# A decoder trunk on one core: up projections of three feed-forwards by seven block products instead of eight

## The chip, the cores and the metric

One core of a Trainium2 chip runs the whole kernel. The metric is the device time of one execution in microseconds. The engines are TensorE (PE in the profile; PEld is its weight load), VectorE (DVE), ScalarE (ACT), GpSimd (POOL) and SyncE (SP), whose queue issues nearly all transfers.

## The reference

256 rows of 1024 numbers go through two layers, all in 32-bit floats:

```
x += 1/2 * SwiGLU_1(RMSNorm(x))          # w_ffn1: up 1024 x 5632, down 2816 x 1024
x += W_o(gated sum of three mixers of RMSNorm(x))
x += 1/2 * SwiGLU_2(RMSNorm(x))          # w_ffn2, the same sizes
x += sigmoid(RMSNorm(x) W_pg) * (p W_pp)
```

and a final RMSNorm. `SwiGLU(h)`: `g, u = split(h @ w_up)`, then `(silu(g) * u) @ w_down`. There are so four feed-forwards: w_ffn1 and w_ffn2 in layers 0 and 1.

## The kernel before

Products are made of three matmuls each (`mm3`): every operand is split into a hi part, rounded to the format fp32r, and a lo part, what the rounding left over; hi x hi, hi x lo and lo x hi are added up in PSUM. A weight unit is a tile of 128 x 1024 numbers, 512 KB: `fetch` brings it into a buffer of the pool wraw (four), `split_unit` makes hi on ScalarE (a copy, L201) and lo on VectorE (a subtraction, L202), in the pools wh and wl, five buffers each. For rows the transposed x is kept in hi and lo (`xth`, `xtl`), one tile for each half of 128 rows (t = 0, 1).

A feed-forward runs over 11 blocks (FB) of 256 gate and 256 value columns. A block has four up units q, each with two slices of 128 of the 1024 inner numbers. For each t it makes 4 x 2 x 3 = 24 up matmuls with 512 columns into one PSUM bank (pool pu, two banks). Then `hid` takes Silu of the gate half on ScalarE (L308) and multiplies it by the value half on VectorE (L309); both apply rstd there, the row factor of the norm, as x itself was transposed without it. The down matmuls of the block before follow (24, into four acc banks that stay for the whole feed-forward), then four transposes of the hidden block and its split into hi and lo (L214, L215; tiles fh and fl). The first and the last block go through t = 0 wholly before t = 1, the others alternate.

`square_linear` is the 1024 x 1024 product behind the mixers (w_out) and the one in the ple step (w_ple_gate); its `consume` adds to x (L954, L415). `norm_after` follows: transposes of raw x (L234), gain with hi and lo (L217, L218), sums of squares (L277), and rstd as a power on GpSimd (L224).

The instructions are written in program order; a scheduler that knows tiles and buffers lays down each engine's final order when the kernel is built, and puts in every wait. Pools of buffers are all opened once, at the start.

Of the kernel before, what the change touches and what calls it, by code (L numbers as in the profile page):

```python
# [8 lines left out]
F32 = mybir.dt.float32  # L9
F32R = mybir.dt.float32r  # L10
# [51 lines left out]

SPLIT_AHEAD = 0
LANES = {'a': 1, 'b': 1, 'c': 2}


class Packed:
# [9 lines left out]
    def array(self):  # L77
        return np.concatenate(self.parts)


# [7 lines left out]
def pack(w):  # L88
    out = []
    for i in range(DEPTH):  # L90
# [10 lines left out]
        def ffn(f):  # L101
            up = w[f + "_up"][i].reshape(4, 2, 128, 2, FB, 256)
            for b in range(FB):
                for q in range(4):
                    p.put((f + "_up", b, q), up[q, :, :, :, b, :].reshape(2, 128, 512))
                for g in range(2):
                    p.put((f + "_down", b, g), rows(f + "_down", b * 256 + g * 128, 1, 0, 1024))
# [22 lines left out]
class Build:  # L130
# [73 lines left out]

    def mm3(self, out, ah, al, bh, bl, start, stop):
        mm = self.nc.tensor.matmul
        mm(out, ah, bh, start=start, stop=False)  # L207
        mm(out, ah, bl, start=False, stop=False)  # L208
        mm(out, al, bh, start=False, stop=stop)  # L209

# [40 lines left out]
    def norm_begin_early(self, gcol):  # L251
        self.next = gcol

    def norm_after(self, t, half):
        if half == 0:
            return
        if t == 0:
            self.norm_begin(self.next)
        for h in range(2):
            self.norm_half(t, h)  # L260
            if self.gcol is None:
                s = slice(h * 512, (h + 1) * 512)
                o = self.tmt("o")
                self.nc.vector.tensor_tensor(o, self.x[:, t, s], self.gf[:, s], op=OP.mult)
                self.og[t].append(o)
        self.norm_finish(t)

    def norm_half(self, t, half):
# [19 lines left out]
    def ffn(self, name, gcol_next, mid=None, hook=None):  # L288
        nc = self.nc
        rstd = self.rstd  # L290
        acc = {}

# [12 lines left out]
        def hid(pu, t):  # L305
            sg = self.tm.tile([128, 256], F32, name="sg", tag="tm")
            hd = self.tm.tile([128, 256], F32, name="hd", tag="tm")
            nc.scalar.activation(sg, pu[t][:, 0, :], AF.Silu, scale=rstd[t])  # L308
            nc.vector.scalar_tensor_tensor(hd, pu[t][:, 1, :], rstd[t], sg, op0=OP.mult, op1=OP.mult)  # L309
            return hd  # L310
# [12 lines left out]
        prev = None  # L323
        for b in range(FB):
            pu = [self.pu.tile([128, 2, 256], F32, name="pu") for t in range(2)]
# [15 lines left out]
            for q, t in order:  # L341
                up(q, t)
            hds = [hid(pu, t) for t in range(2)]
            if b < FB - 1:
                if prev is not None:
                    d = down_units(b - 1)
                    for t in range(2):
                        down(b - 1, d, prev, t, b == 1, False)
                pt = self.pt.tile([128, 2, 256], F32, name="pt")
# [3 lines left out]
            else:  # L353
# [9 lines left out]
                turn(0)  # L363
                down(b - 1, d0, prev, 0, False, False)
# [4 lines left out]
                down(b - 1, d0, prev, 1, False, False)  # L369
# [4 lines left out]
            prev = (hh, ll)  # L374

# [545 lines left out]
    def mixer(self, i, gcol_next):  # L921
# [30 lines left out]
        def consume(t, half, ps):  # L952
            xs = self.x[:, t, half * 512:(half + 1) * 512]
            nc.vector.tensor_tensor(xs, xs, ps, op=OP.add)  # L954
            self.norm_after(t, half)

        self.norm_begin_early(gcol_next)
        self.square_linear("w_out", consume)
# [59 lines left out]
    def program(self, out):  # L1018
# [34 lines left out]
        for i in range(DEPTH):  # L1053
            self.layer = i
            self.ffn("w_ffn1", cols["norm_mix"] + 8 * i, hook=self.late_loads if i == 0 else None)
            self.mixer(i, cols["norm_ffn2"] + 8 * i)
            self.ffn("w_ffn2", cols["norm_ple"] + 8 * i, mid=lambda: self.ple_proj(i))
            if i + 1 == DEPTH:
                self.gf = self.ar1.tile([128, 1024], F32, name="gf", tag="ar1a")
# [3 lines left out]
            self.ple(i, cols["norm_ffn1"] + 8 if i + 1 < DEPTH else None)  # L1063
        for t in range(2):
# [12 lines left out]

def build(nc, aps, out, where):
    from contextlib import ExitStack
    with tile.TileContext(nc) as tc, ExitStack() as es:  # L1080
# [40 lines left out]
```

## Time and profile before

| | us |
|---|---|
| median of three runs | 1531.94 (1531.2 to 1532.58) |
| the profiled execution | 1531.52 |
| its span, first to last instruction | 1529.7 |
| TensorE busy | 1507.0 |
| VectorE busy | 946.2 |
| ScalarE busy | 860.9 |

The page gives busy times by engine, slices of the span, a chain of work that ended last, groups of instructions by source line, and transfers. Matmuls overlap one another, so the duration of one (0.39 us) is longer than the step from one to the next. A line such as L202 can be that of a helper that many stages call. The four feed-forwards lie at about 15 to 200, 560 to 740, 770 to 955 and 1306 to 1490 us of the span.

### The profile page before, as it was taken

What the parts mean: (1) busy time and instruction counts of PE and PEld (TensorE: products, weight loads), DVE (VectorE), ACT (ScalarE), POOL (GpSimd) and SP (SyncE); (2) the same over time, 40 slices, a digit from 0 to 9 for tenths busy, and PEclk for the clock granted to TensorE, in tenths of its full rate; (3) what the DMA queues carried; (4) which work ended last, traced back from release to release, by engine and by line L of the source; (5) the groups of instructions that cost most, each with busy time, mean ns of one, the idle gap of its engine ahead of it and who ended that gap; (6) DMA issues with size and microseconds to landing.
All of it is one profiled execution on the core that took longest, in us unless ns stands there. A gap on an engine that the chain in (4) does not pass through costs nothing.

```text
span 1529.7 us, 21640 instructions
## 1 busy us (share of the span) xinstructions
PE 1507.0 (99%) x8264; PEld 1256.8 (82%) x8264; DVE 946.2 (62%) x1534; ACT 860.9 (56%) x1313; POOL 36.3 (2%) x48
## 2 busy tenths in 40 slices
PE   7999999999999999999999999999999999999997
PEld 6888888888888888888888888888888888888886
DVE  6555577677765665555765456676776566655456
ACT  6444486568655464444764445865775644644455
POOL 0000010000000000000000000100000000000000
PEclk9999999999999999999999999999999999999999
DMA  8565545344535556565565555554353365566652
GB/s 296 187 195 191 185 140 187 123 159 138 172 110 166 192 191 184 180 196 172 184 198 190 191 181 159 183 160 134 126 186 126 127 204 190 174 195 187 190 172 97
DMA packets 76472, 264.54 MB, mean 173 GB/s; under 512 B 8608, under 2 KB 9536, under 8 KB 76368
## 3 DMA queue, kind: packets, MB, share of 16 engines
q1 hardware_dynamic: 76144, 263.00, 53.8%
q8 instruction: 65, 1.06, 0.3%
q0 software_dynamic: 80, 0.11, 0.1%
q14 instruction: 39, 0.32, 0.1%
q10 hardware_dynamic: 144, 0.05, 0.0%
HBM read 262.08 MB, written 1.05 MB: 172 GB/s over the span
## 4 chain that ended last, share of the span: by engine, by line
PE 89%; ACT 5%; DVE 2%; DMA 1%; issue 1%; POOL 0%; SPq 0%; POOLq 0%; ACTq 0%; DVEq 0%
PE pu L207 20%; PE pu L208 20%; PE pu L209 20%; PE acc L209 5%; PE acc L208 5%; PE acc L207 5%; PE sq L207 2%; PE sq L208 2%; PE sq L209 2%; ACT h L201 1%; PE pt L314 1%; DMA raw<-in_weights_dram 1%; PE pt L234 1%; DVE l L202 1%; ACT P L513 1%
## 5 line engine op out<-in xcount | busy, mean ns | idle before, releaser
L202 DVE TENSOR_TENSOR l<-raw,h 128x1024 fp32r<-128x1024 f32 (+3 forms) x512 | 600.0, 1185 | 388.7 <-ACT h L201 382.7
L201 ACT CAST h<-raw 128x1024 fp32r<-128x1024 f32 (+1 forms) x511 | 512.9, 1016 | 375.5 <-PE pu L209 240.0
L207 PE MATMUL pu<-h,xth 128*128 128x512 f32 (+3 forms) x1376 | 534.6, 389 | 8.0 <-DVE h L201 5.9
L208 PE MATMUL pu<-l,xth 128*128 128x512 f32 (+3 forms) x1376 | 526.2, 382 | 2.1 <-DVE l L202 2.1
L209 PE MATMUL pu<-h,xtl 128*128 128x512 f32 (+3 forms) x1376 | 523.5, 381 | 0.0
L207 PEld LDWEIGHTS pu<-h,xth 128*128 128x128 f32 x1376 | 259.4, 189 | 54.6 <-ACT xth L217 5.9
L208 PEld LDWEIGHTS pu<-l,xth 128*128 128x128 f32 x1376 | 259.5, 189 | 46.6 <-DVE l L202 4.8
L209 PEld LDWEIGHTS pu<-h,xtl 128*128 128x128 f32 x1376 | 259.1, 188 | 45.6
L207 PE MATMUL acc<-h,fh 128*128 128x512 f32 x352 | 138.0, 392 | 0.0
L209 PE MATMUL acc<-h,fl 128*128 128x512 f32 x352 | 137.6, 391 | 0.0
L208 PE MATMUL acc<-l,fh 128*128 128x512 f32 x352 | 137.1, 389 | 0.0
L308 ACT ACTIVATE sg<-pu,rstd 128x256 f32<-128x256 f32 x88 | 41.8, 475 | 63.9 <-PE pu L209 63.9
L209 PEld LDWEIGHTS acc<-h,fl 128*128 128x128 f32 x352 | 66.1, 188 | 13.6
L208 PEld LDWEIGHTS acc<-l,fh 128*128 128x128 f32 x352 | 66.1, 188 | 13.4
L207 PEld LDWEIGHTS acc<-h,fh 128*128 128x128 f32 x352 | 66.1, 188 | 13.2
L309 DVE SCALAR_TENSOR_TENSOR hd<-pu,rstd,sg 128x256 f32<-128x256 f32 x88 | 42.3, 481 | 38.7 <-ACT sg L308 38.7
L208 PE MATMUL pu<-l,fh 128*128 128x512 f32 x128 | 50.8, 397 | 0.0
L207 PE MATMUL sq<-h,xth 128*128 128x512 f32 x128 | 50.4, 394 | 0.0
L207 PE MATMUL pu<-h,fh 128*128 128x512 f32 x128 | 50.3, 393 | 0.0
L209 PE MATMUL sq<-h,xtl 128*128 128x512 f32 x128 | 50.0, 391 | 0.0
L208 PE MATMUL sq<-l,xth 128*128 128x512 f32 x128 | 50.0, 391 | 0.0
L217 ACT ACTIVATE xth<-pt,gains 128x128 fp32r<-128x128 f32 x112 | 37.3, 367 | 22.5 <-PE pt L234 11.3
(228 smaller groups left out, 1364.6 us busy)
## 6 DMA issues: line engine op xcount, KB each, us to landing
raw<-in_weights_dram SPq DMA_DIRECT2D x446, 512.0 KB, 4.2
raw<-in_weights_dram SPq DMA_DIRECT2D x48, 384.0 KB, 3.1
raw<-in_weights_dram SPq DMA_DIRECT2D x8, 320.0 KB, 3.0
raw<-in_weights_dram SPq DMA_DIRECT2D x8, 256.0 KB, 2.7
xin<-in_xt_dram SPq DMA_DIRECT2D x4, 256.0 KB, 7.3
x<-in_x_dram SPq DMA_DIRECT2D x2, 512.0 KB, 9.9
out_dram<-o SPq DMA_DIRECT2D x4, 256.0 KB, 2.2
cf<-in_const_f_dram SPq DMA_DIRECT2D x1, 864.0 KB, 8.3
```

The source lines that it names most:

```text
L201: (copy or nc.scalar.copy)(h[:, :m], raw[:, :m])
L202: nc.vector.tensor_tensor(l[:, :m], raw[:, :m], h[:, :m].bitcast(F32), op=OP.subtract)
L207: mm(out, ah, bh, start=start, stop=False)
L208: mm(out, ah, bl, start=False, stop=False)
L209: mm(out, al, bh, start=False, stop=stop)
L217: nc.scalar.activation(h, src, AF.Copy, scale=gain)
L234: nc.tensor.transpose(pt[:, k, :], src[:, half * 512 + k * 128:half * 512 + (k + 1) * 128], self.ident)
L308: nc.scalar.activation(sg, pu[t][:, 0, :], AF.Silu, scale=rstd[t])
L309: nc.vector.scalar_tensor_tensor(hd, pu[t][:, 1, :], rstd[t], sg, op0=OP.mult, op1=OP.mult)
L314: nc.tensor.transpose(pt[:, f, t * 128:(t + 1) * 128], hd[:, f * 128:(f + 1) * 128], self.ident)
L513: nc.scalar.activation(P[n, o], P[n, o], AF.Exp, bias=q[:, 3:4], scale=A_SCALE, accum_out=q[:, 4 + n:5 + n])
```

## The change

In w_ffn2 of both layers and w_ffn1 of layer 1, blocks 1 and 2, 4 and 5, 7 and 8 are joined: a double block is a product of x (two halves of rows, and even and odd slices of 128 of the inner numbers) with weights whose halves are likewise the even and odd slices, and block b and b + 1's 512 + 512 columns as they lie in memory (lo and hi halves of a 1024-wide row). Strassen's method in Winograd's form makes the 2 x 2 product out of seven block products: four sums of x (`sums_x`, once for each feed-forward, behind block 0), four sums of weights (`add`, in place on the raw tiles), and seven `prod`, each of 12 matmuls; three of them gather in the bank pa, whose state in between is copied out (`keep`). Each product makes its own hi and lo parts of its two weight tiles. Weights of a double block come as eight transfers of 512 KB into four tiles of 128 x 2 x 1024 (pools we and wo, two buffers each).

As sums of x mix rows, rstd must be in x before: `scaled_xt` multiplies x by rstd, transposes, multiplies by the gains, and keeps that raw tile for the sums; it stands behind the sum of squares and the power. `hid` then needs no rstd. The pools of the mixers and those of double blocks are opened and closed in turn, on the same memory. w_ffn1 of layer 0 stays as it was, and blocks 0, 3, 6, 9 and 10 of the others are single. The transfer of gf gets a pool of its own. A double block's hidden parts are transposed after the down matmuls of the block before; the next block has down matmuls for two.

```diff
+WIDE = (1, 4, 7)
+def plan(name, i):
+    if (name, i) == ("w_ffn1", 0):
+        return [(False, b) for b in range(FB)]
+    return [(b in WIDE, b) for b in range(FB) if b - 1 not in WIDE]
...
     def norm_after(self, t, half):
+        self.norm_sum(t, half)
+        if self.gcol is None:
+            s = slice(half * 512, (half + 1) * 512)
+            o = self.tmt("o")
+            self.nc.vector.tensor_tensor(o, self.x[:, t, s], self.gf[:, s], op=OP.mult)
+            self.og[t].append(o)
         if half == 0:
             return
-        if t == 0:
-            self.norm_begin(self.next)
-        for h in range(2):
-            self.norm_half(t, h)
...
         self.norm_finish(t)
+        if self.gcol is not None:
+            if t == 0:
+                self.new_xt()
+                self.wide_open()
+            self.scaled_xt(t)
+
+    def scaled_xt(self, t):
+        nc = self.nc
+        raw = self.xr.tile([128, 8, 128], F32, name=f"xr{t}", tag=f"xr{t}")
+        self.rawx[t] = raw
+        xs = [self.tmt("xs") for half in range(2)]
+        nc.scalar.activation(xs[0], self.x[:, t, 0:512], AF.Copy, scale=self.rstd[t])
+        nc.vector.tensor_scalar(xs[1], self.x[:, t, 512:1024], self.rstd[t], None, op0=OP.mult)
+        for half in range(2):
+            pt = self.pt.tile([128, 4, 128], F32, name="pt")
+            for k in range(4):
+                nc.tensor.transpose(pt[:, k, :], xs[half][:, k * 128:(k + 1) * 128], self.ident)
+            c = self.gcol + half * 4
+            g = slice(half * 4, half * 4 + 4)
+            nc.vector.tensor_tensor(raw[:, g, :], pt, self.gains[:, c:c + 4].unsqueeze(2).to_broadcast([128, 4, 128]),
+                                    op=OP.mult)
+            self.hl(self.xth[t][:, g, :], self.xtl[t][:, g, :], raw[:, g, :])
+
+    def wide_open(self):
+        self.scope = ExitStack()
+        for n, bufs in (("we", 2), ("wo", 2), ("xr", 1), ("sx", 1)):
+            setattr(self, n, self.scope.enter_context(self.tc.tile_pool(name=n, bufs=bufs, reuse_waits="tile")))
+        self.rawx = [None, None]
...
+    def sums_x(self):
+        nc = self.nc
+        a = [r.rearrange("p (q k) t -> p q k t", k=2) for r in self.rawx]
+        (a11, a12), (a21, a22) = [(r[:, :, 0, :], r[:, :, 1, :]) for r in a]
+        s1, s2, s3, s4 = [self.tmt("xs").rearrange("p (q t) -> p q t", q=4) for j in range(4)]
+        nc.vector.tensor_tensor(s1, a22, a21, op=OP.subtract)
+        nc.vector.scalar_tensor_tensor(s2, s1, -1.0, a11, op0=OP.mult, op1=OP.subtract)
+        nc.vector.tensor_tensor(s3, a11, a21, op=OP.subtract)
+        nc.vector.scalar_tensor_tensor(s4, a12, -1.0, s2, op0=OP.mult, op1=OP.subtract)
+        self.sx_ = []
+        for j, v in enumerate((s1, s2, s3, s4)):
+            h = self.sx.tile([128, 4, 128], F32R, name=f"sh{j}", tag=f"sh{j}")
+            l = self.sx.tile([128, 4, 128], F32R, name=f"sl{j}", tag=f"sl{j}")
+            self.hl(h, l, v)
+            self.sx_.append((h, l))
...
+    def wide_up(self, name, b):
+        nc = self.nc
+        e, o = self.wide_fetch(name, b)
+        lo, hi = slice(0, 512), slice(512, 1024)
+        pb = self.pu.tile([128, 512], F32, name="pu")
+        pa = self.pu.tile([128, 512], F32, name="pu")
+        pc = self.pt.tile([128, 512], F32, name="pt")
...
+        def prod(ps, st, raws, half, start, stop):
+            for j in range(2):
+                h = self.wh.tile([128, 1024], F32R, name="h").rearrange("p (q n) -> p q n", q=2)
+                l = self.wl.tile([128, 1024], F32R, name="l").rearrange("p (q n) -> p q n", q=2)
+                src = raws[j][:, :, half]
+                nc.scalar.copy(h, src)
+                nc.vector.tensor_tensor(l, src, h.bitcast(F32), op=OP.subtract)
+                for q in range(2):
+                    self.mm3(ps, st[0][:, 2 * j + q, :], st[1][:, 2 * j + q, :], h[:, q, :], l[:, q, :],
+                             start and j == 0 and q == 0, stop and j == 1 and q == 1, True)
+
+        def add(d, dh, r, rh):
+            for j in range(2):
+                nc.vector.tensor_tensor(d[j][:, :, dh], d[j][:, :, dh], r[j][:, :, rh], op=OP.add)
+
+        def keep(ps):
+            c = self.tmt("pc")
+            nc.scalar.copy(c, ps)
+            return c
+
+        mul = nc.vector.scalar_tensor_tensor
+        prod(pa, a11, e, lo, True, False)
+        p1 = keep(pa)
+        add(e, lo, e, hi)
+        prod(pb, s1, e, lo, True, False)
+        p5 = keep(pb)
+        add(e, lo, o, hi)
+        prod(pa, s2, e, lo, False, False)
+        u2 = keep(pa)
+        prod(pb, s4, o, hi, False, True)
+        nc.vector.tensor_tensor(u2, u2, pb, op=OP.add)
+        add(e, hi, o, hi)
+        prod(pa, s3, e, hi, False, False)
+        u3 = keep(pa)
+        prod(pc, a12, o, lo, True, True)
+        nc.vector.tensor_tensor(p1, p1, pc, op=OP.add)
+        nc.scalar.activation(p1, p1, AF.Silu)
+        mul(u2, u2, -1.0, p1, op0=OP.mult, op1=OP.mult)
+        add(e, lo, o, lo)
+        prod(pa, a22, e, lo, False, True)
+        nc.vector.tensor_tensor(p5, p5, u3, op=OP.add)
+        nc.scalar.activation(u3, pa, AF.Silu)
+        mul(p5, p5, -1.0, u3, op0=OP.mult, op1=OP.mult)
+        return [u2, p5]
...
+        for wide, b in plan(name, self.layer):
+            if wide:
+                hds = self.wide_up(name, b)
+                downs()
+                prev = []
+                for j in range(2):
+                    hh = self.fh.tile([128, 2, 256], F32R, name="fh")
+                    ll = self.fl.tile([128, 2, 256], F32R, name="fl")
+                    pt = self.pt.tile([128, 2, 256], F32, name="pt")
+                    for t in range(2):
+                        hid_t(pt, hds[t][:, j * 256:(j + 1) * 256], t)
+                    self.hl(hh, ll, pt)
+                    prev.append((b + j, (hh, ll)))
+                continue
...
             hds = [hid(pu, t) for t in range(2)]
+            if scaled and b == 0:
+                self.sums_x()
...
-POOLS = dict(wraw=4, wh=5, wl=5, act=1, const=1, tm=6, small=4, fh=4, fl=4, ar1=1, ar2=1, pp_=3, gt=6)
+POOLS = dict(wraw=4, wh=5, wl=5, act=1, const=1, tm=6, small=4, fh=4, fl=4)
```

Below, W1 to W14 are the 14 weight tiles that the seven products split, in order.

## Rows read from the trace of the kernel before

**Rows 1.** The page's busy times by engine, and the granted clock in 40 slices of the span (9 is 90% or more).

```profile
PE 1507.0 (99%) x8264; PEld 1256.8 (82%) x8264; DVE 946.2 (62%) x1534; ACT 860.9 (56%) x1313; POOL 36.3 (2%) x48
PEclk9999999999999999999999999999999999999999
```

**Rows 2.** Windows inside three of the four feed-forwards: start and end, length, busy time of each engine with instructions, granted clock, DMA share, GB/s.

```profile
20.00:190.00 170.00, 170.00 (x772) 140.61 (x771) 92.21 (x97) 79.41 (x97) 0.00 (x0) 1.00 0.61 197
560.00:730.00 170.00, 170.00 (x772) 140.56 (x771) 91.16 (x96) 77.52 (x94) 0.00 (x0) 1.00 0.61 190
...
1330.00:1480.00 150.00, 150.00 (x680) 124.15 (x679) 77.22 (x80) 66.87 (x80) 0.00 (x0) 1.00 0.60 183
```

**Rows 3.** The page's groups by line: shapes and count, busy us, mean ns of one, then idle time of the engine before them and what ended it.

```profile
L202 DVE TENSOR_TENSOR l<-raw,h 128x1024 fp32r<-128x1024 f32 (+3 forms) x512 | 600.0, 1185 | 388.7 <-ACT h L201 382.7
L207 PE MATMUL pu<-h,xth 128*128 128x512 f32 (+3 forms) x1376 | 534.6, 389 | 8.0 <-DVE h L201 5.9
```

**Rows 4.** The window of one block of w_ffn2 in layer 1, from its first up matmul to that of the next block; columns as in rows 2.

```profile
1385.32:1402.13 16.81, 16.81 (x80) 13.91 (x78) 8.74 (x9) 7.53 (x10) 0.00 (x0) 1.00 0.61 187
```

**Rows 5.** TensorE's timeline of that block: start, duration, operation; the first and last of 48 up matmuls and of 24 down matmuls (x1 each, a few records missing), the transposes, the next block's first.

```profile
1385.32 0.48 PE L207 MATMUL pu<-h,xth 128*128 128x512 f32 x1
...
1396.11 0.39 PE L209 MATMUL pu<-h,xtl 128*128 128x512 f32 x1
1396.33 0.39 PE L207 MATMUL acc<-h,fh 128*128 128x512 f32 x1
...
1401.55 0.39 PE L209 MATMUL acc<-h,fl 128*128 128x512 f32 x1
1401.78 0.60 PE L314 MATMUL pt<-ident,hd 128*128 128x128 f32 x4
1402.13 0.48 PE L207 MATMUL pu<-h,xth 128*128 128x512 f32 x1
```

**Rows 6.** VectorE's timeline: two lo parts of the next block and fl behind them, one that waits; then two 512-wide operations in a row from a mixer, and three lo parts in a row from the ple step. In brackets the idle time before, and who ended it.

```profile
1385.56 2.36 DVE L202 TENSOR_TENSOR l<-raw,h 128x1024 fp32r<-128x1024 f32 x2 [3.17 <-ACT h L201]
1387.84 0.68 DVE L215 TENSOR_TENSOR fl<-pt,fh 128x512 fp32r<-128x512 f32 x1
1389.46 1.23 DVE L202 TENSOR_TENSOR l<-raw,h 128x1024 fp32r<-128x1024 f32 x1 [0.94 <-ACT h L201]
...
1169.12 0.68 DVE L658 TENSOR_TENSOR e<-e,pt 128x512 f32<-128x512 f32 x1
1169.72 0.68 DVE L659 TENSOR_TENSOR sig<-sig,pt 128x512 f32<-128x512 f32 x1
...
1508.12 3.49 DVE L202 TENSOR_TENSOR l<-raw,h 128x1024 fp32r<-128x1024 f32 x3
```

**Rows 7.** ScalarE's timeline over the same block.

```profile
1384.48 2.00 ACT L201 CAST h<-raw 128x1024 fp32r<-128x1024 f32 x2 [3.35 <-PE acc L209]
1386.38 0.58 ACT L214 CAST fh<-pt 128x512 fp32r<-128x512 f32 x1
1388.37 1.05 ACT L201 CAST h<-raw 128x1024 fp32r<-128x1024 f32 x1 [1.42 <-PE pu L209]
```

**Rows 8.** The timeline of all engines at the end of w_out in layer 1: transposes of raw x, the addition to x of t = 0, its square, sum, mean and power, two of ScalarE's casts, and the last matmul of t = 1.

```profile
1299.45 0.60 PE L234 MATMUL pt<-ident,x 128*128 128x128 f32 x4
1299.65 0.69 DVE L954 TENSOR_TENSOR x<-x,sq 128x512 f32<-128x512 f32 x1 [2.71 <-PE sq L209]
1300.37 0.63 ACT L277 ACTIVATE jk<-x 128x512 f32<-128x512 f32 x1
1301.12 0.16 DVE L282 TENSOR_TENSOR s<-ss 128x1 f32<-128x1 f32 x1 [0.29 <-ACT jk L277]
1301.55 0.56 POOL L224 TENSOR_TENSOR rstd<-ms,mhalf 128x1 f32<-128x1 f32 x1 [118.27 <-DVE ms L223]
1304.06 2.03 ACT L201 CAST h<-raw 128x1024 fp32r<-128x1024 f32 x2
1305.67 0.39 PE L209 MATMUL sq<-h,xtl 128*128 128x512 f32 x1
```

**Rows 9.** The timeline at the end of the ple gate in layer 0, t = 0: sigmoid, product, addition to x, and the power.

```profile
760.32 0.69 ACT L413 ACTIVATE g<-sq,rstd 128x512 f32<-128x512 f32 x1 [3.76 <-PE sq L209]
761.04 0.69 DVE L414 TENSOR_TENSOR g<-g,pp 128x512 f32<-128x512 f32 x1 [2.39 <-ACT g L413]
761.91 0.68 DVE L415 TENSOR_TENSOR x<-x,g 128x512 f32<-128x512 f32 x1
765.53 1.54 POOL L224 TENSOR_TENSOR rstd<-ms,mhalf 128x1 f32<-128x1 f32 x1 [21.00 <-ACT h L201]
```

**Rows 10.** Transfers of weight units (count, KB each, median us from issue to landing), and a window at the start of the kernel (columns as in rows 2).

```profile
raw<-in_weights_dram SPq DMA_DIRECT2D x446, 512.0 KB, 4.2
10.00:15.00 5.00, 3.35 (x7) 2.36 (x8) 3.80 (x9) 4.43 (x8) 0.00 (x0) 1.00 1.04 412
```

**Rows 11.** TensorE's timeline at the start of the kernel.

```profile
11.18 0.79 PE L207 MATMUL pu<-h,xth 128*128 128x512 f32 x1 [1.61 <-ACT h L201]
...
14.32 0.63 PE L209 MATMUL pu<-h,xtl 128*128 128x512 f32 x1
14.74 0.63 PE L207 MATMUL pu<-h,xth 128*128 128x512 f32 x1
...
16.10 0.40 PE L208 MATMUL pu<-l,xth 128*128 128x512 f32 x1
16.34 0.40 PE L209 MATMUL pu<-h,xtl 128*128 128x512 f32 x1
```

More of the change, by code (lines that the diff above doesn't have):

```diff
@@ L1 @@
+from contextlib import ExitStack
 import numpy as np
@@ L102, in ffn @@
             up = w[f + "_up"][i].reshape(4, 2, 128, 2, FB, 256)
+            for wide, b in plan(f, i):
+                if wide:
+                    for k in range(2):
+                        for q in range(4):
+                            p.put((f + "_wide", b, 4 * k + q), up[q, k, :, :, b:b + 2, :].reshape(1, 128, 1024))
+                else:
+                    for q in range(4):
+                        p.put((f + "_up", b, q), up[q, :, :, :, b, :].reshape(2, 128, 512))
             for b in range(FB):
-                for q in range(4):
-                    p.put((f + "_up", b, q), up[q, :, :, :, b, :].reshape(2, 128, 512))
                 for g in range(2):
@@ L252, in norm_begin_early @@
         self.next = gcol
+        self.gcol = gcol
+        self.ss = [self.small.tile([128, 2], F32, name="ss", tag="ss") for t in range(2)]
+        self.rstd = [self.small.tile([128, 1], F32, name="rstd", tag="rstd") for t in range(2)]
     def norm_after(self, t, half):
+        self.norm_sum(t, half)
[4 more added lines that the diff above has]
+            self.og[t].append(o)
@@ new lines, in wide_open, with mixer_open @@
+    def wide_open(self):
[3 more added lines that the diff above has]
+        self.rawx = [None, None]
+    def mixer_open(self):
+        self.scope = ExitStack()
+        for n, bufs in (("ar1", 1), ("ar2", 1), ("pp_", 3), ("gt", 6)):
+            setattr(self, n, self.scope.enter_context(self.tc.tile_pool(name=n, bufs=bufs, reuse_waits="tile")))
@@ new lines, in wide_fetch @@
+    def wide_fetch(self, name, b):
+        out = []
+        for k, pool in enumerate((self.we, self.wo)):
+            for j in range(2):
+                raw = pool.tile([128, 2, 1024], F32, name="wide", tag="wide")
+                for q in range(2):
+                    off, _, m = self.where[self.layer][name + "_wide", b, 4 * k + 2 * j + q]
+                    self.nc.sync.dma_start(raw[:, q, :], self.a[f"weights{self.layer}"][off:off + 128 * m]
+                                           .rearrange("(p m) -> p m", p=128))
+                out.append(raw)
+        return out[:2], out[2:]
@@ L290, in ffn @@
         rstd = self.rstd
+        scaled = (name, self.layer) != ("w_ffn1", 0)
         acc = {}
@@ L323, in ffn, with downs @@
         prev = None
-        for b in range(FB):
+        def downs():
+            for (pb, hT) in prev:
+                d = down_units(pb)
+                for t in range(2):
+                    down(pb, d, hT, t, pb == 0, False)
+        for wide, b in plan(name, self.layer):
+            if wide:
+                hds = self.wide_up(name, b)
+                downs()
+                prev = []
+                for j in range(2):
+                    hh = self.fh.tile([128, 2, 256], F32R, name="fh")
+                    ll = self.fl.tile([128, 2, 256], F32R, name="fl")
+                    pt = self.pt.tile([128, 2, 256], F32, name="pt")
+                    for t in range(2):
+                        hid_t(pt, hds[t][:, j * 256:(j + 1) * 256], t)
+                    self.hl(hh, ll, pt)
+                    prev.append((b + j, (hh, ll)))
+                continue
             pu = [self.pu.tile([128, 2, 256], F32, name="pu") for t in range(2)]
@@ L343, in ffn @@
             hds = [hid(pu, t) for t in range(2)]
+            if scaled and b == 0:
+                self.sums_x()
             if b < FB - 1:
                 if prev is not None:
-                    d = down_units(b - 1)
-                    for t in range(2):
-                        down(b - 1, d, prev, t, b == 1, False)
+                    downs()
                 pt = self.pt.tile([128, 2, 256], F32, name="pt")
@@ L363, in ffn @@
                 turn(0)
-                down(b - 1, d0, prev, 0, False, False)
+                old = prev[0][1]
+                down(b - 1, d0, old, 0, False, False)
                 turn(1)
@@ L368, in ffn @@
                 finish(0)
-                down(b - 1, d0, prev, 1, False, False)
+                down(b - 1, d0, old, 1, False, False)
                 down(b, d1, (hh, ll), 1, False, True)
```

37 lines of the change are left out of this document (23 added, 14 removed).

## The prediction

> **What bounds the kernel now.** I read the page's head first: TensorE is busy for 99% of the span at a granted clock of 0.9 or more in every slice, VectorE 62%, ScalarE 56% [rows 1]. Then the windows of the feed-forward stretches: TensorE is busy 170 of 170 us and 150 of 150 us there, VectorE about half [rows 2]. So inside a feed-forward the stream of matmuls sets the time, and a matmul left out is time gained, as long as its operands are still there in time. The groups by line say who comes next: VectorE's lo parts wait for ScalarE's hi parts, TensorE waits 8 us in all for a hi part, and that over the whole kernel [rows 3]. Next I took one 256-column block apart. It is 16.81 us long, of which VectorE works 8.74 [rows 4]: 48 up matmuls, 24 down matmuls, 4 transposes [rows 5]. From the first down matmul to the last are 23 steps in 5.22 us, 0.227 us each [rows 5]. VectorE and ScalarE sit waiting for TensorE to release a buffer: wh and wl hold five units, and each next hi part starts only when a matmul has ended [rows 6, 7]. These five buffers are the whole lead that the two engines can have.
>
> **What is removed.** A double block is 2 blocks x 48 = 96 up matmuls; seven products of 12 are 84. Nine double blocks (three in each of three feed-forwards) save 9 x 12 x 0.227 = 24.5 us [rows 5]. Down matmuls and transposes keep their number.
>
> [...] The trace shows 227 ns [rows 5], and the sum goes by the trace.
>
> **What is added to VectorE, per double block.** Before, the up part needed 8 lo parts. Now each of the 7 products splits its own two 1024-column tiles: 14 lo parts; and the weight sums take 8 additions of the same shape. A lo part lasts 1.22 us alone, but two in a row take 2.36 and three 3.49, so one more costs 1.14 [rows 6]. The additions are the same operation on the same shape, read in pieces of 512, and I cost them alike: 22 x 1.14 = 25.1 us. Four half-size operations (fl of the block before, u2+pb, p1+pc, p5+u3) stand ahead of the last split; two 512-wide ones in a row start 0.60 us apart [rows 6]: 2.4 us. Together 27.5 us of VectorE against 84 x 0.227 = 19.1 us of TensorE. In these stretches VectorE is the longer one. Over a double block with the block behind it, it isn't: VectorE has about 27.5 + 2 multiplications 1.2 + 2 down lo parts 2.3 + 2 fl 1.2, then 8 lo parts 9.1 + 2 hd 0.9 + fl, some 43 us; TensorE 84 + 24 + 48 + 48 matmuls, 46.3 us, and 1.5 of transposes. So everything hangs on how much of the 27.5 us is done before the first product starts.
>
> [...] With the full 1.22 us for each of 22 operations a double block would cost an estimated 1.8 us more, 16 us over nine. The rows show 1.14 from start to start, and I stay with them.
>
> **Later double blocks (six).** Ahead of one stand the 48 down matmuls of a pair of blocks. In the last 24 of them (5.4 us) and the 0.5 us of transposes two of five buffers still serve the downs, three are free. VectorE then can do W1, W2, the first two additions and W3, five operations, 5.7 us: it starts 5.9 us early. Its last split is ready at 27.5 - 5.9 = 21.6 us after the first product's start; 6 matmuls follow, 1.4 us: 23.0 against 19.1, a stall of 3.9 us. Better: e hi += o hi depends on no buffer, only on the first additions, and one buffer may be free earlier still; 2.7 us more lead leave 1.2. Worse: no lead at all, 9.8. The order on each engine is laid down when the kernel is built, and the rows of before show that it runs ahead as far as buffers allow (two next splits ahead of fl) [rows 6, 7], so I take 2.5: 6 x 2.5 = 15 us.
>
> **First double blocks (three).** No downs stand between block 0 and the first product, all four up units of block 0 stay in use until its second row half, and sums_x adds 4 sums and 4 lo parts, 8 x 0.6 = 4.8 us of VectorE, just there. Of 5.9 us of lead 1.1 are left: 27.5 - 1.1 + 1.4 - 19.1 = 8.7 us. Between 6.5 (a split slipped in before the sums) and 9.8 I take 8: 3 x 8 = 24 us.
>
> **Rows scaled beforehand (three boundaries).** Before, transposes took raw x, and rstd was needed only at the Silu. Now the chain is x, Square, sum, mean, power, scaling, transposes, gain, hi, lo. Behind w_out the rows give 2.46 us from the addition's start to the end of the power [rows 8]; then scaling 0.69 (as the scaled sigmoid [rows 9]), transposes 0.60 [rows 8], gain 0.68 (as fl [rows 6]), hi 0.58 [rows 7]: 5.0 us, lo 0.7 more. It is covered by the 24 matmuls of the second row half, 5.4 us, but casts of 1.0 us stand on the same ScalarE queue, as two do in those rows [rows 8]. Bounds 0 to 2, I take 1. Behind the ple gate sigmoid, product and addition come first, 2.3 us from 760.32 to 762.6 [rows 9]: 2.3 + (2.46 - 0.69) + 2.55 = 6.6 us, and 1.0 more with the power at the 1.54 us that it took there [rows 9]; against 5.4 and with a cast I take 2.5. Together 2 x 1 + 2.5 = 4.5 us, between 1 and 8. The final norm's earlier Square saves nothing: x is late there, not the sum.
>
> **Costed at nothing.** ScalarE: 14 casts at 0.96 (two take 2.00, one 1.05 [rows 7]), 4 evacuations and 2 Silus make some 17 us of 23; it keeps step, since a cast runs beside the second addition. If not, its delay is VectorE's, inside the upper bound. DMA: the bytes are the same, 8 transfers of 512 KB per pair. e and o have one set of buffers, so the next pair's transfers start when the last split of this one is done, some 30 us ahead of use, with 8 others on SP's queue: 16 x 512 KB in 30 us are 280 GB/s; 412 were moved in a stretch of the start [rows 10]. Cover gone, see below. The evacuations of pa and pb are each covered by a product on the other bank (2.7 us). Pools opened later overlay tiles last read before w_out.
>
> **Sum.** -24.5 + 15 + 24 + 4.5 = +19 us. The profiled execution took 1531.52 us (span 1529.7 and 1.8 around it), 0.4 below the runs' median of 1531.94: 1550.5, say **1550 us**. The parts at their good ends give 6 x 1.2 + 3 x 6.5 + 1 - 24.5 = +3 (1535), at their bad ends 6 x 3.9 + 3 x 9.8 + 8 - 24.5 = +36 (1568).
>
> **Rivals.**
> *Faster: the lead is enough.* The surplus of VectorE is 8.4 us per double block; if the scheduled order hides it all (additions and splits early, in the block before, where VectorE idles half the time [rows 4]), only sums_x (4.8 each) and 1 to 3 us of boundaries remain: -24.5 + 14.4 + 2 = -8, 1523 us. It decides at a mean stall below (24.5 - 4.5) / 9 = 2.2 us. Against it: five buffers [rows 6, 7]. Chance 0.17 for a gain of over 0.2%, which is 3 us and about what the runs can tell.
> *Nothing measurable*, within 3 us of 1532: good ends nearly throughout. 0.09.
> *Slower as forecast*, 1535 to 1570: 0.58.
> *No lead*: engine order puts evacuations ahead of casts, so that ScalarE waits for TensorE in each product and VectorE's lead is gone; 9 x 9.8 + 4.5 - 24.5 = +68, 1600 us. Against it: the rows run ahead now [rows 7]. 0.09.
> *e and o late*: SP holds the 8 wide transfers behind units that wait for buffers. If the first product waits 4 us each time: 1550 + 36 = 1586. Median landing is 4.2 us [rows 10]. 0.04.
> *Clock*: at the start, after idle time and with gaps of 1.6 us among them, matmuls stood 0.42 us apart, half speed, and 0.24 after an unbroken run [rows 11]. If the stalls brought that back for 10 us in each double block, 9 x 5 = 45 us more, 1595. The stalls forecast are shorter and lie between runs of 1.4 us or more. 0.03. [...]
>
> Faster 0.17, same 0.09, slower 0.74. The range leaves out gains of over 6 us and the rivals above 1575, some 2 in 10: **1525 to 1572**.
>
> **What will show it.** 108 matmuls fewer on TensorE's pu groups; in double blocks VectorE busy over nine tenths and TensorE's waits on l of the wide splits, 1 to 4 us in all per later pair, 6 to 10 in a first one, most in the last products (behind e lo += o lo); the normal blocks between at 22.3 us without waits; TensorE waiting up to 3 us at block 0. The prediction is wrong if the additions take well under 1.14 us, if the lead is much longer than three buffers, or if TensorE's waits name a DMA or an evacuation.

## The result, and the profile after

The changed kernel took 1550.84 us (median of four runs, 1547.79 to 1551.78), the kernel before, beside it, 1531.57: a ratio of 1.0121, 95% interval 1.0104 to 1.0139. It is slower by 19.3 us. The sum said +19 and 1550; but that it met the number is luck: three of its terms were off, one by -11, one by +7 and one by +4 us, as the experiments show. The profiled execution took 1551.78 us, its span is 1550.0.

The page's busy times and granted clock of the kernel after answer to [rows 1]:

```profile
PE 1503.8 (97%) x8156; PEld 1239.6 (80%) x8156; DVE 1113.9 (72%) x1675; ACT 925.6 (60%) x1367; POOL 37.2 (2%) x48
PEclk9999999999999999999979999999999999999999
```

The 108 matmuls are gone (8264 before, 8156 now), VectorE has 168 us more, and one slice has a lower granted clock. The groups by line give the splits of wide tiles and the additions, then the splits that are left:

```profile
L217 DVE TENSOR_TENSOR l<-raw,h 128x1024 fp32r<-128x1024 f32 (+3 forms) x440 | 512.1, 1179 | 237.6 <-ACT h L216 229.5
L361 DVE TENSOR_TENSOR l<-wide,h 128x1024 fp32r<-128x1024 f32 x126 | 148.3, 1220 | 11.6 <-ACT h L360 11.4
L368 DVE TENSOR_TENSOR wide<-wide 128x1024 f32<-128x1024 f32 x72 | 85.8, 1220 | 0.4
```

126 is 9 x 14 and 72 is 9 x 8, and an addition costs what a split costs, 1.22 us alone, as the sum had it. Before them VectorE idles 0.4 and 11.6 us in all: beside the wide work it idles little. What TensorE waited for in the whole kernel (us in all, times, longest):

```profile
PE pu L223 <- DVE l L361: 7.4, 7, 1.9
PE pu L222 <- DVE h L216: 6.0, 1, 6.0
PE pu L224 <- DVE sl L230: 5.0, 3, 1.8
PE pt L298 <- ACT xs L293: 2.9, 3, 1.2
```

The second is the kernel's start, which was there before [rows 3]. New are the lo parts of wide tiles, the lo parts of the sums of x, and the scaled rows. Nine pairs, but seven waits for wide lo parts: six lie in the three first pairs. Three windows show why: a first pair in w_ffn2 of layer 0, a later pair of the same, the first pair in w_ffn1 of layer 1 (columns as in rows 2):

```profile
570.00:583.00 13.00, 8.58 (x27) 5.59 (x27) 13.00 (x15) 8.46 (x13) 0.00 (x0) 0.87 0.00 1
621.90:647.20 25.30, 25.15 (x111) 19.98 (x109) 24.78 (x26) 18.57 (x23) 0.00 (x0) 1.00 0.38 137
790.00:810.00 20.00, 15.17 (x43) 10.54 (x42) 16.28 (x20) 10.50 (x17) 0.00 (x0) 0.66 0.00 1
```

In the later pair VectorE is busy 24.78 of 25.30 us, and TensorE is busy 25.15: the surplus exists, and costs TensorE nearly nothing. In the first pair of w_ffn2 VectorE works all 13.00 us, TensorE 8.58 of them, and the mean granted clock is 0.87; in w_ffn1 of layer 1 it is 0.66, and there VectorE works only 16.28 of 20.00 us. VectorE's timeline ahead of that later pair and in it:

```profile
613.03 1.22 DVE L361 TENSOR_TENSOR l<-wide,h 128x1024 fp32r<-128x1024 f32 x1
614.28 2.49 DVE L368 TENSOR_TENSOR wide<-wide 128x1024 f32<-128x1024 f32 x2
616.69 2.36 DVE L361 TENSOR_TENSOR l<-wide,h 128x1024 fp32r<-128x1024 f32 x2
618.96 3.49 DVE L368 TENSOR_TENSOR wide<-wide 128x1024 f32<-128x1024 f32 x3
622.37 2.36 DVE L361 TENSOR_TENSOR l<-wide,h 128x1024 fp32r<-128x1024 f32 x2
...
635.05 4.62 DVE L361 TENSOR_TENSOR l<-wide,h 128x1024 fp32r<-128x1024 f32 x4
```

and TensorE's at the first product and at its longest delay in the products:

```profile
621.88 0.48 PE L222 MATMUL pu<-h,xth 128*128 128x512 f32 x1
...
631.56 0.61 PE L222 MATMUL pu<-h,sh 128*128 128x512 f32 x2
632.32 0.50 PE L223 MATMUL pu<-l,sh 128*128 128x512 f32 x1
```

The first product starts at 621.88, VectorE began at 613.03: 8.85 us of lead, in which seven operations are done, four of them additions, and a fifth addition is under way. The other later pairs have 9.1 to 9.7 us. The prediction's three splits are there, but the additions that need no buffer were put around them, more of them than the prediction had moved. The delay at 631.56 is 0.3 us (0.76 where two steps would be 0.45).

In the first pair of that feed-forward VectorE's line is this, from the sums of x on:

```profile
569.27 0.69 DVE L322 SCALAR_TENSOR_TENSOR xs<-xs,xr 128x512 f32<-128x512 f32 x1
...
571.07 2.50 DVE L230 TENSOR_TENSOR sl<-xs,sh 128x512 fp32r<-128x512 f32 x4
...
574.08 2.35 DVE L361 TENSOR_TENSOR l<-wide,h 128x1024 fp32r<-128x1024 f32 x2
576.35 3.49 DVE L368 TENSOR_TENSOR wide<-wide 128x1024 f32<-128x1024 f32 x3
579.76 2.36 DVE L361 TENSOR_TENSOR l<-wide,h 128x1024 fp32r<-128x1024 f32 x2
```

and TensorE's beside it:

```profile
571.82 0.50 PE L224 MATMUL pu<-h,sl 128*128 128x512 f32 x1 [1.61 <-DVE sl L230]
...
575.36 0.50 PE L223 MATMUL pu<-l,sh 128*128 128x512 f32 x1 [1.89 <-DVE l L361]
...
577.13 0.63 PE L224 MATMUL pu<-h,sl 128*128 128x512 f32 x1
577.56 0.63 PE L222 MATMUL pu<-h,sh 128*128 128x512 f32 x1
...
581.04 0.50 PE L223 MATMUL pu<-l,sh 128*128 128x512 f32 x1 [0.78 <-DVE l L361]
```

TensorE waits for the sums' lo parts, then for a split behind them, then for one behind three additions. Between, at 577.13 and 577.56, its matmuls stand 0.43 us apart, where 0.23 is the step in [rows 5]: half speed, at a granted clock of 0.50 (576.70 to 579.00), after waits of 1.6 and 1.9 us.

In w_ffn1 of layer 1 more stands in the way. These are the end of TensorE's second product, ScalarE's copy of its result (`keep`) with the casts behind it, VectorE's next split, and TensorE's next product:

```profile
799.90 0.63 PE L224 MATMUL pu<-h,sl 128*128 128x512 f32 x1
800.57 0.58 ACT L372 COPY pc<-pu 128x512 f32<-128x512 f32 x1 [4.36 <-PE pu L224]
801.05 4.83 ACT L360 CAST h<-wide 128x1024 fp32r<-128x1024 f32 x5
802.13 5.77 DVE L361 TENSOR_TENSOR l<-wide,h 128x1024 fp32r<-128x1024 f32 x5 [1.61 <-ACT h L360]
802.15 0.79 PE L222 MATMUL pu<-h,sh 128*128 128x512 f32 x1 [1.62 <-ACT h L360]
```

The second product runs mostly at half speed (steps of 0.43 us from 796.49 on, a granted clock of 0.50 from 795 to 800), the copy waits 4.36 us for its end, and five casts stand behind the copy in ScalarE's order, so that VectorE and TensorE both wait for a cast. VectorE waits so once more, 2.23 us, at 810.13.

The starts of the four `square_linear` (first sq matmul in TensorE's timeline) cut the kernel into stretches, in us:

| | to w_out of layer 0 | w_out and w_ffn2 | ple, w_ffn1, mixers | w_out and w_ffn2 | rest |
|---|---|---|---|---|---|
| before | 527.3 | 216.4 | 539.0 | 216.4 | 30.7 |
| after | 527.9 | 220.3 | 550.9 | 220.3 | 30.5 |
| difference | +0.6 | +4.0 | +11.9 | +4.0 | -0.2 |

The stretch with w_ffn1 of layer 1 loses three times what the others lose; it has the ple gate's longer chain, the lowest clock (0.66 from 790 to 810), and the casts that come late.

### The profile page after: what moved, and what is told of

It reads as the page before. It is cut to its first block, busy times and chain, and to the rows that moved or that the text cites. A ratio compares the mean times of both kernels' runs of the same rounds, so it can differ in the third digit from the quotient of the medians.

```text
span 1550.0 us, 21601 instructions
## 1 busy us (share of the span) xinstructions
PE 1503.8 (97%) x8156; PEld 1239.6 (80%) x8156; DVE 1113.9 (72%) x1675; ACT 925.6 (60%) x1367; POOL 37.2 (2%) x48
## 4 chain that ended last, share of the span: by engine, by line
PE 81%; DVE 9%; ACT 6%; issue 2%; DMA 1%; POOL 1%; SPq 0%; POOLq 0%; DVEq 0%; ACTq 0%
PE pu L223 18%; PE pu L224 17%; PE pu L222 17%; PE acc L223 5%; PE acc L224 5%; PE acc L222 5%; DVE l L361 3%; DVE l L217 2%; PE sq L223 2%; PE sq L222 2%; PE sq L224 2%; ACT h L216 1%; DMA raw<-in_weights_dram 1%; DVE wide L368 1%; PE pt L451 1%
## 5 line engine op out<-in xcount | busy, mean ns | idle before, releaser
L217 DVE TENSOR_TENSOR l<-raw,h 128x1024 fp32r<-128x1024 f32 (+3 forms) x440 | 512.1, 1179 | 237.6 <-ACT h L216 229.5
L216 ACT CAST h<-raw 128x1024 fp32r<-128x1024 f32 (+4 forms) x439 | 438.6, 1011 | 248.1 <-PE pu L224 124.8
L222 PE MATMUL pu<-h,xth 128*128 128x512 f32 (+3 forms) x1160 | 450.3, 389 | 10.9 <-DVE h L216 6.0
L223 PE MATMUL pu<-l,xth 128*128 128x512 f32 (+3 forms) x1160 | 443.5, 382 | 3.8 <-DVE l L217 2.1
L224 PE MATMUL pu<-h,xtl 128*128 128x512 f32 (+3 forms) x1160 | 441.1, 381 | 1.7 <-DVE xtl L230 1.7
L360 ACT CAST h<-wide 128x1024 fp32r<-128x1024 f32 x126 | 126.3, 1050 | 55.6 <-PE acc L224 40.5
L361 DVE TENSOR_TENSOR l<-wide,h 128x1024 fp32r<-128x1024 f32 x126 | 148.3, 1220 | 11.6 <-ACT h L360 11.4
L368 DVE TENSOR_TENSOR wide<-wide 128x1024 f32<-128x1024 f32 x72 | 85.8, 1220 | 0.4
L223 PE MATMUL pu<-l,sh 128*128 128x512 f32 x144 | 60.1, 417 | 6.6 <-DVE l L361 5.9
L224 PE MATMUL pu<-h,sl 128*128 128x512 f32 x144 | 59.7, 414 | 5.0 <-DVE sl L230 5.0
```

What stands on the lines that cost most here:

```text
L216: (copy or nc.scalar.copy)(h[:, :m], raw[:, :m])
L217: nc.vector.tensor_tensor(l[:, :m], raw[:, :m], h[:, :m].bitcast(F32), op=OP.subtract)
L222: mm(out, ah, bh, start=start, stop=False, skip_group_check=skip)
L223: mm(out, ah, bl, start=False, stop=False, skip_group_check=skip)
L224: mm(out, al, bh, start=False, stop=stop, skip_group_check=skip)
L360: nc.scalar.copy(h, src)
```

## The experiments

All times are medians beside runs of the kernel before on the same chip (1531.8 to 1532.3 us), with the ratio and its 95% interval.

| kernel | us | ratio | interval |
|---|---|---|---|
| scaled_only | 1540.19 | 1.0052 | 1.0037 to 1.0067 |
| late_pairs | 1527.80 | 0.9974 | 0.9963 to 0.9986 |
| first_pair | 1565.05 | 1.0213 | 1.0198 to 1.0228 |
| no_adds | 1528.38 | 0.9975 | 0.9963 to 0.9986 |
| no_sums | 1535.26 | 1.0022 | 1.0013 to 1.0032 |
| pairs_2_5 | 1532.17 | 1.0003 | 0.9994 to 1.0013 |
| late_norm_first | 1528.28 | 0.9975 | 0.9965 to 0.9985 |
| late_one_mean | 1528.68 | 0.9977 | 0.9968 to 0.9986 |
| late_four_buffers | 1556.22 | 1.0159 | 1.0145 to 1.0173 |
| before_four_buffers | 1540.99 | 1.0057 | 1.0042 to 1.0073 |
| scaled_no_wait | 1534.29 | 1.0016 | 1.0006 to 1.0025 |

Theory A is the prediction with its terms. Theory B, formed from the trace after, has the same mechanisms but puts the loss on first pairs and boundaries.

**The three terms one by one.** scaled_only:

```diff
-WIDE = (1, 4, 7)
+WIDE = ()
...
-            if scaled and b == 0:
+            if scaled and b == 0 and WIDE:
```

> Edit: no double block at all, and no sums of x; rows are still scaled before the up projections. Theory A (the prediction's terms: boundaries 4.5 us in all, first pairs 8 us each, later pairs 2.5 us each): before + 4.5 = 1536 us. Theory B (read from the trace after: later pairs cost about 0.4 us, boundaries 3 to 8 us each, because small operations of the norm queue behind weight work on VectorE and ScalarE, and TensorE's clock falls): before + 8 to 13 = 1540 to 1545 us if ordinary splits delay the norm as much, some 1537 if only the wide splits do.

late_pairs:

```diff
-WIDE = (1, 4, 7)
+WIDE = (4, 7)
```

> Edit: pairs at blocks 4 and 7 alone, block 1 and 2 single; sums of x kept. Against scaled_only: theory A 6 x (2.5 - 2.7) = -1 us, so about the same time; theory B 6 x (0.4 - 2.7) = -14 us and the sums of x hidden behind blocks 1 to 3, so 1523 to 1531 us.

first_pair:

```diff
-WIDE = (1, 4, 7)
+WIDE = (1,)
```

> Edit: the pair at block 1 alone in each of the three feed-forwards. Against scaled_only: theory A 3 x (8 - 2.7) = +16 us; theory B 2 x (7 - 2.7) + (12 - 2.7) = +18 us, the more the longer the clock stays low behind block 0.

Scaled rows alone cost 8.2 us, not 4.5. Six later pairs on top of that make it 12.4 us faster: they save 6 x 2.72 = 16.3 and give back 3.9, that is 0.65 us each with the sums of x, not 2.5. Three first pairs on top of it make it 24.9 us slower, more than either theory said: they save 8.2 and lose 33.0, 11.0 us each on average, not 8. Put together, 1540.2 - 12.4 + 24.9 = 1552.7, the change took 1550.8: the terms add up within 2 us. So theory B's figures held for the scaled rows and the later pairs, theory A's for neither.

The stretches of the table above, taken in the profiled executions of these kernels, tell where the terms lie. scaled_only is longer than the kernel before by 2.0, 4.2 and 2.0 us in the second, third and fourth stretch. The change is longer than late_pairs by 6.1, 11.8 and 6.1 us (220.3, 550.9 and 220.3 against 214.2, 539.1 and 214.2); with the 2.7 us that each saves, a first pair costs 8.8 us in either w_ffn2 and 14.5 in w_ffn1 of layer 1.

The change without its first pairs beats both kernels: late_pairs is 4.2 us faster than the kernel before, 23 us faster than the change.

**What makes a first pair slow.** no_adds:

```diff
-                nc.vector.tensor_tensor(d[j][:, :, dh], d[j][:, :, dh], r[j][:, :, rh], op=OP.add)
+                nc.vector.tensor_tensor(d[j][:, 0, dh][:, 0:8], d[j][:, 0, dh][:, 0:8], r[j][:, 0, rh][:, 0:8], op=OP.add)
```

> Edit: the eight additions of weights in each pair are cut to 8 columns of 1024, so the products use wrong weights and the output is not the reference's; everything else stays. Theory A: VectorE's 27.5 us fall to some 19, no surplus is left in any pair: 1531.5 - 24.5 + 4.5 and little for the first pairs, 1512 to 1516 us. Theory B: the later pairs gain under 0.5 us each (3 us in all), the first pairs lose the additions that stand between their splits but keep the sums of x (4.8 us each) and the boundaries: 1528 to 1536 us.

no_sums:

```diff
-        s1, s2, s3, s4 = self.sx_
+        s1 = s2 = s3 = s4 = (xh[1][:, :, 0, :], xl[1][:, :, 0, :])
...
-            if scaled and b == 0:
-                self.sums_x()
```

> Edit: pairs at 1, 4 and 7 as in the change, but the sums of x and their hi and lo parts are left out and a slice of x stands in their place, so the output is not the reference's. A first pair costs 8.3 us net, 11 us of waiting, by first_pair against scaled_only. If that is VectorE work alone, the sums' 4.8 us each go: 14 us, 1536 to 1538 us. If the sums come late because their inputs come late (the rows' second half) and the low clock follows from that wait, more goes: 1528 to 1534 us. If the additions alone make it, under 6 us: above 1544 us.

Without the additions the change loses 22.5 us of its time, and its 1528.4 lie in theory B's range, far above theory A's; the later pairs can't have given more than the 3.9 that they cost, so the first pairs gave 18.6 or more, some 6.2 each, of the 8 x 1.14 = 9.1 us of VectorE's work that the additions were. Without the sums it loses 15.6 (1535.3, just below the range for VectorE's work alone), 5.2 each on average, near the 4.8 us that the sums keep VectorE busy; but by stretch it is 4.0, 9.8 and 2.5 us. Work taken from VectorE comes back as time, in w_ffn2 in part, in w_ffn1 of layer 1 twice over. There the granted clock without the sums is 1.00 from 785 to 812 us, where the change has 0.66 from 790 to 810: with the sums go their waits, and the slow matmuls and late casts behind these. The runs do not separate the low clock from VectorE's work.

pairs_2_5:

```diff
-WIDE = (1, 4, 7)
+WIDE = (2, 5)
```

> Edit: two pairs in each feed-forward, at blocks 2 and 5 instead of 4 and 7, so that one single block with its down matmuls stands between block 0 and the first pair. If the first pair suffers only from standing directly behind block 0 (sums of x just made, no down matmuls for cover), one block is enough and the time is that of late_pairs, 1526 to 1530 us. If the first transfers or the new memory of the pools make it slow, it stays 3 x 4 us or more above: 1540 us.

Neither: 4.4 us above late_pairs, 1.5 for each feed-forward. One single block between gives the first pair its down matmuls for cover, and most of the 11 us go; but not all of it. TensorE's waits for wide lo parts come to 4.0 us in that run:

```profile
PE pu L223 <- DVE l L361: 4.0, 6, 1.4
```

With pairs at 4 and 7 that line is not among the longest. Fewer down matmuls ahead (24, not 48) are not the reason: the pair at block 4 in late_pairs also has 24, and TensorE waits for none of its lo parts. What differs is the lead. The first split starts 9.95 us before the first product in late_pairs, and 8.1 us before it in w_ffn2 of layer 0 in pairs_2_5 (574.53 and 582.63), where VectorE's timeline has no idle time from 564 us to the pair's end: it is still busy with the splits and sums of block 0.

**What a later pair's lead rests on.** late_four_buffers and before_four_buffers:

```diff
-POOLS = dict(wraw=4, wh=5, wl=5, ...
+POOLS = dict(wraw=4, wh=4, wl=4, ...
```

> Edit: late_pairs with four instead of five buffers in each of wh and wl. Theory A (the lead of a pair is what the five buffers allow): one split less ahead, 1.1 us or more per pair, 7 us or more beyond what four buffers cost the kernel before (before_four_buffers). Theory B (the lead of a later pair is carried by the additions, which need no buffer in wh and wl and are put early): the cost of four buffers is that of the kernel before, within 3 us.

> Edit: the kernel before with four instead of five buffers in each of wh and wl; the yardstick for late_four_buffers. VectorE is busy half of the time in the feed-forwards, and the next split starts when a unit's 12 matmuls (2.7 us) end; one buffer less leaves cover: both theories expect 1531 to 1545 us.

One buffer fewer costs the kernel before 8.7 us and late_pairs 28.4. The 19.7 between are 3.3 us for each of six pairs. TensorE's waits for wide lo parts in late_four_buffers, and in the last of its pairs VectorE's first split, TensorE's first product and its first wait:

```profile
PE pu L223 <- DVE l L361: 13.3, 12, 1.8
```

```profile
1436.36 2.36 DVE L361 TENSOR_TENSOR l<-wide,h 128x1024 fp32r<-128x1024 f32 x2 [3.27 <-ACT h L360]
1441.55 0.48 PE L222 MATMUL pu<-h,xth 128*128 128x512 f32 x1
1449.59 0.50 PE L223 MATMUL pu<-l,sh 128*128 128x512 f32 x1 [1.77 <-DVE l L361]
```

The lead is 5.19 us here and 7.2 in the first pair of each feed-forward; with five buffers, in late_pairs, it is 9.7 to 9.95.

So theory B's reading of the later pairs fails here, and theory A's holds: the lead is set by the buffers, additions pulled ahead or not. Five are just enough, four are not. More than five was not tried.

**Scaled rows.** late_norm_first:

```diff
     def norm_after(self, t, half):
+        with self.tc.high_priority():
+            self.norm_now(t, half)
+
+    def norm_now(self, t, half):
...
```

> Edit: pairs at blocks 4 and 7 as in late_pairs, and the operations of the norm (square, sum, power, scaling, transposes, gain, hi and lo) get a higher priority when the order is laid down, so that they go ahead of weight splits. If the 8.2 us that scaled rows cost alone (1540.2 against 1532.0) come from small operations of the norm standing behind weight work in a queue, most of it goes: 1522 to 1525 us. If the chain from x to the first hi part is itself too long for its cover of 5.4 us, little changes: 1526 to 1528 us.

Nothing changed, but the order on VectorE hadn't either, so it decides nothing. Its timeline at the end of w_out in layer 0 is that of late_pairs, later by 0.1 us or less. Here late_pairs:

```profile
553.52 0.68 DVE L1112 TENSOR_TENSOR x<-x,sq 128x512 f32<-128x512 f32 x1
554.12 1.22 DVE L217 TENSOR_TENSOR l<-raw,h 128x1024 fp32r<-128x1024 f32 x1
555.26 0.15 DVE L414 TENSOR_TENSOR s<-ss 128x1 f32<-128x1 f32 x1
555.33 1.22 DVE L217 TENSOR_TENSOR l<-raw,h 128x1024 fp32r<-128x1024 f32 x1
556.46 0.14 DVE L238 TENSOR_SCALAR ms<-s 128x1 f32<-128x1 f32 x1
557.28 0.49 DVE L294 TENSOR_SCALAR xs<-x,rstd 128x512 f32<-128x512 f32 x1 [0.68 <-POOL rstd L239]
```

with the power on GpSimd:

```profile
556.69 0.56 POOL L239 TENSOR_TENSOR rstd<-ms,mhalf 128x1 f32<-128x1 f32 x1 [8.29 <-DVE ms L238]
```

From the addition to x to the end of the power it is 3.73 us. This is the second half of the rows, t = 1. The 2.46 us of [rows 8] are those of the first half, and the first half has not become longer: in scaled_only it has 2.47. In the kernel before the second half took longer still, 5.26 us at this place, and nothing waited for it ahead of the Silu:

```profile
551.45 0.68 DVE L954 TENSOR_TENSOR x<-x,sq 128x512 f32<-128x512 f32 x1
556.15 0.56 POOL L224 TENSOR_TENSOR rstd<-ms,mhalf 128x1 f32<-128x1 f32 x1 [9.34 <-DVE ms L223]
```

In late_pairs a weight split stands ahead of the sum and another between sum and mean; that is about the 1.27 us by which the two halves differ. late_one_mean takes one of these places away:

```diff
-        nc.scalar.activation(jk, xs, AF.Square, accum_out=self.ss[t][:, half:half + 1])
+        nc.scalar.activation(jk, xs, AF.Square, scale=1.0 / 32, accum_out=self.ss[t][:, half:half + 1])
...
-        nc.vector.tensor_tensor(s1, self.ss[t][:, 0:1], self.ss[t][:, 1:2], op=OP.add)
-        self.rsqrt(self.rstd[t], s1, DM, 1)
+        nc.vector.tensor_scalar(ms, self.ss[t][:, 0:1], self.ss[t][:, 1:2], EPS, op0=OP.add, op1=OP.add)
+        nc.gpsimd.tensor_tensor(self.rstd[t], ms, self.mhalf[:, :1], op=OP.pow)
```

> Edit: late_pairs, and the two small VectorE operations between square and power (sum of two halves, then mean with epsilon) made one, with the 1/1024 put into the Square. late_norm_first changed nothing since its VectorE order stayed: in both, a weight split of 1.2 us stands before the sum and another between sum and mean. If these places in the queue make the boundaries slow, one passage less saves about 1.1 us at each of three boundaries: 1524 to 1526 us. If the chain's own length makes it, 0.2 us each: 1527 to 1528 us.

No gain. VectorE's timeline and the power say where it went:

```profile
553.02 0.68 DVE L1112 TENSOR_TENSOR x<-x,sq 128x512 f32<-128x512 f32 x1
...
554.75 0.21 DVE L414 TENSOR_SCALAR ms<-ss 128x1 f32<-128x1 f32 x1
554.88 1.22 DVE L217 TENSOR_TENSOR l<-raw,h 128x1024 fp32r<-128x1024 f32 x1
```

```profile
555.04 1.47 POOL L415 TENSOR_TENSOR rstd<-ms,mhalf 128x1 f32<-128x1 f32 x1 [7.15 <-DVE ms L414]
```

The mean is earlier by one split, but the power now runs beside that split and ends only after it: 1.47 us, where it took 0.56 with VectorE idle. The way from the addition to the power is 3.49 us, 0.24 shorter. So the last experiment took the wait itself away, scaled_no_wait:

```diff
-        nc.scalar.activation(xs[0], self.x[:, t, 0:512], AF.Copy, scale=self.rstd[t])
-        nc.vector.tensor_scalar(xs[1], self.x[:, t, 512:1024], self.rstd[t], None, op0=OP.mult)
+        nc.scalar.activation(xs[0], self.x[:, t, 0:512], AF.Copy, scale=self.mhalf[:, 0:1])
+        nc.vector.tensor_scalar(xs[1], self.x[:, t, 512:1024], self.mhalf[:, 0:1], None, op0=OP.mult)
```

> Edit: scaled_only, but rows are scaled by a constant column instead of rstd, so the output is not the reference's; square, sum, mean and power still run, every other operation of the scaled path too, only nobody waits for the power. late_one_mean took one passage through VectorE's queue away and gained nothing, since the power on GpSimd then ran beside a weight split and lasted 1.47 instead of 0.56 us. If the wait for sum, mean and power makes the 8.2 us of scaled_only: 1532 to 1534 us. If the added operations themselves make it (scaling, gain apart from hi and lo, 512 wide steps in place of 128 wide ones): 1537 to 1541 us.

The 1534.3 lie just above the range for the wait. Of 8.2 us 5.9 go with the wait for rstd, 2.3 stay with the operations. So the wait for the chain is the cause of most of it. That weight splits stand between its small steps is read from the timeline; what they cost of the 5.9 is not shown, as no run took both out of the way.

## Why the prediction was right, and where its terms were not

**The direction, the bound and the sum.** In the first pairs VectorE took TensorE's place as the limit, as forecast: an addition costs what a split costs, and TensorE waits for lo parts. In the later pairs VectorE is as busy as forecast (26.7 to 27.5 us from the first split to the end of the last, where the sum had 27.5), but TensorE stays the limit. The saving is as worked out, 108 matmuls. The total, +19, is right because three errors cancel, and that is luck.

| term | predicted | measured | from |
|---|---|---|---|
| later pairs | +15 | +3.9 | late_pairs against scaled_only |
| first pairs | +24 | +31.2 | the change against late_pairs, with 8.2 saved |
| boundaries | +4.5 | +8.2 | scaled_only against before |
| saving | -24.5 | -24.5 | 108 matmuls at 0.227 |
| sum | +19 | +18.8 | the change: +19.3 |

The three differences add up to the change by the way they are taken; the check on them is first_pair, measured by itself, with 2 us left over.

**Later pairs** were mis-sized. The mechanism held (take a buffer away and 3.3 us per pair appear), but the step from lead to stall was too careful: 5.9 us of lead and "2.7 us more" were the two ends, I took a stall of 2.5 between them, and the lead was 8.85 to 9.7, a little beyond the good end, whose stall of 1.2 became 0.65. A lead much longer than three buffers was one of the prediction's own signs of being wrong. The rows that showed the order running ahead of the program [rows 6, 7] spoke for the good end, and I went to the middle. The check named for it (1 to 4 us of waits per later pair, most of them in the last products) came out wrong: 0.3 us, in the middle of the pair.

**First pairs** were mis-sized the other way, 10.4 us each in the change and 11.0 alone. By place, the two in w_ffn2 cost 8.8, near the 8 assumed, and nearly all of the +7 lies in w_ffn1 of layer 1 with 14.5. The two causes named, no down matmuls for cover and 4.8 us of sums, are what the runs show. Missing were the order, which puts three additions ahead of the split that TensorE waits for at 581.04, the clock, and for w_ffn1 the casts behind the copy at 800.57: that is the mechanism of the rival *No lead* (0.09), in one pair of nine. How the 14.5 divide among these is not shown. The check named for it, 6 to 10 us of waits on the wide lo parts, came out lower: 1.89 and 0.78 us in the pair shown, 4.4 with its waits for the sums' lo part and for a cast.

**The clock** was a rival at 3 in 100 with 45 us, reasoned away because the stalls would be short. It came in small: the clock was low behind waits of under 2 us, near one another, in the first pairs (0.50 from 576.7 to 579, behind 1.61 and 1.89 us) and at one boundary (behind 0.53, 0.59 and 0.95 us). In the profiled execution the windows at 0.87 and 0.66 hold at most 13 x 0.13 = 1.7 and 20 x 0.34 = 6.8 us, less what TensorE waited anyway; the first pair of w_ffn2 in layer 1 (0.72 from 1347 to 1353 us) and the boundary at the ple gate (0.76 from 773 to 780) hold at most 1.7 each. The mean granted clock was 0.991 there and 0.994 to 0.995 in the other three runs, where before had 0.998; those three took 0.9 to 4.0 us less, but two of them at the same 0.995 took 1547.79 and 1550.76 us: what the clock costs in a run is not shown. In the trace the low stretches have steps of 0.43 us, the others 0.23.

**Boundaries** were mis-sized: 5.9 us of waiting and 2.3 of work; 2.0 us at each w_out, where 1 was taken, and 4.2 at the ple gate, where 2.5 was. The step that failed is the chain's length. It was taken from [rows 8], the first half of the rows; what TensorE waits for is the second half's, 3.73 us in place of 2.46, with two weight splits of VectorE in its way. GpSimd's power was not the cause in scaled_only, where it took 0.55 to 0.56 us at every boundary, at the ple gate too, where the prediction had 1.54. In the change it took 1.53 in the second half of both w_out, beside a weight addition: that is a cost of the first pairs.

**Faster, and e and o late.** The rival's turning point, a mean stall below 2.2 us, was passed by the later pairs but missed by the first ones: that rival was true of six pairs of nine. No wait of TensorE names a wide transfer; ScalarE's casts of ordinary units waited 63 us for transfers, after 8 before, and that cost TensorE nothing that its own waits show.

## What to carry to other kernels

A change that pays TensorE with VectorE's time is to be judged place by place: the same surplus of VectorE cost 0.65 us where other matmuls gave it a lead, and 9 to 15 us where none stood ahead. So leave out the places without cover before giving up the change; here six of nine pairs, put where other work stands ahead and VectorE has caught up, beat the kernel that nine pairs made slower by 4 us. And read a chain's length in the half that is waited for. When a term lies between two ends, look at which end the trace's order already speaks for: the sum may come out right without its parts.

## What the runs showed of the hardware that was not expected

GpSimd's power of 128 x 1 took 0.56 us with VectorE idle (late_pairs), 1.47 beside a split (late_one_mean) and 1.53 beside an addition of weights (the change), and beside these it ended 0.4 us after VectorE's operation: at 556.51 after 556.10 in late_one_mean, at 557.19 after 556.78 in the change. Not every operation of VectorE goes with that: the 0.56 us at 1301.55 in [rows 8] lie beside its `xtl<-pt,gains,xth` (1301.39 to 1301.99), whose `pt` is in PSUM. What makes the difference no run shows.

TensorE's clock was low behind short waits: after 1.61 and 1.89 us, which ended at 571.82 and 575.36, its matmuls stood 0.43 us apart from 576.7 to 579, at a granted clock of 0.50, and in w_ffn1 of layer 1, where waits of 0.96, 1.78 and 1.62 us followed one another (ended at 793.38, 795.89 and 802.15), a stretch of 20 us had a mean granted clock of 0.66.
